# Value sums of a stick-breaking attention packed into column halves and quarters of the TensorE array

## The chip, the cores and the metric

The kernel runs on one core of one Trainium2 chip. The metric is the device time of one execution in microseconds (us); less is better. Of the engines, TensorE (PE) multiplies matrices, with its weight loads shown apart (PEld); VectorE (DVE), ScalarE (ACT) and GpSimd (POOL) work elementwise, and SyncE (SP) issues the transfers.

## The reference

One inference step of a two-layer decoder trunk, in fp32, for a prompt of 1024 positions and for 8 sample sequences of 8 new positions each, which share one set of weights. The width is 1024. Each layer is a normed token mixer and a SwiGLU channel mixer of width 2816. The mixer of the first layer has a convolution part (width 31, 512 channels) and a stick-breaking attention with 8 heads of 64, whose outputs are concatenated into one output projection. The second layer's mixer (a short convolution and causal pooling) is not touched here.

The attention has no softmax. With `z = q k / 8 + bias` and the strictly causal mask, the weight of key j for a query is `sigmoid(z_j)` times the product of `1 - sigmoid(z_m)` over the later keys m that the query sees. In the reference:

```python
log_1m = jnp.where(mask, jax.nn.log_sigmoid(-z), 0.0)
after = lax.cumsum(log_1m, axis=3, reverse=True) - log_1m
wgt = jnp.exp(jnp.where(mask, jax.nn.log_sigmoid(z) + after, -jnp.inf))
return jnp.einsum('nhqk,nkhd->nqhd', wgt, v)
```

The prompt attends to itself. Each sample attends to 1024 past positions, whose keys and values lie in 8 pages of 128 positions of a paged cache, and to its own new positions. Besides the trunk's output, the keys, values and the last states are returned.

## The kernel before, in words

All 1088 positions (1024 of the prompt, 64 of the samples) lie channel-major: channels on the 128 partitions, positions along the free dimension. They go through the first layer in two groups: GA has positions 0 to 511, GB 512 to 1087, the samples' 64 among them. The large products are made with three matmuls on two-part operands (a rounded high part and the rest) of type float32r; `mm3` (L231) issues them, L235 is their line, and `block` (L311) makes one output tile of them.

**Background flows.** The attention and the convolution are Python generators that are advanced by one piece in each slot of the projections: `block` calls its slot after every two steps of its inner dimension, and `bg` (L341) takes the next piece. A `yield` therefore means: a stretch of projection matmuls goes here. All engines execute their instructions in the order in which they were issued. `flow_ab` runs the convolution and then the attention of GA while GB is projected; `flow_c` runs the attention of GB, and then the convolution of GB and the sample attention in turns, while the output projection and the channel mixer of GA go on.

**Prompt attention** (`attention`, L937). A unit is one head and one tile of 128 queries; there are 32 in each group, in the order of heads and, in a head, from the last query tile to the first. A tile i has i+1 key tiles: 4 to 1 in GA, 8 to 5 in GB. Four stages, each one unit behind the one before:
- `s1` makes the scores. The contraction holds both parts of an operand in 128 rows: a head's 64 rows with the high parts of keys, and the other 64 rows with the low parts; `qa` has the high part of the queries in both halves, and `qz` their low part in the head's 64 rows and zeros in the rest. Two matmuls (L982) for each block of up to 512 keys, then two sigmoids on ACT.
- `s2` multiplies the running products (DVE).
- `s3` transposes the weights in tiles of 128 x 128 (L1011) and copies them to `wt` (ACT).
- `s4` sums values: per key tile one fp32 matmul with the 64 value columns as weights, into `o2` of 64 partitions (L1020), then one ACT copy (L1021).

**Sample attention** (`sample`, L1051). Two samples with 8 heads and 8 positions each fill 128 rows; there are four such pairs `bp`. Keys come in 24 units, in 48 steps of the loop at L1246. In a step, `trans` is called twice for the next step (transposes of three or two key pages, L1115, a copy on ACT and a subtraction on DVE into `kth`, L1119), `score` makes four matmuls (L1138), `score_b` adds the two parts and takes the sigmoids. When a pair is scored, its running products, and the transposes of its weights (L1187, into `wts`), follow in the next steps. They are put on the dictionary `chain`, and `turned` then puts four entries on `pvq`, each of which is two calls of `pv` (L1202).
- `pv(i)` sums the values of one page number of both samples of the pair: two fp32 matmuls (L1210), each of 64 rows of weights' columns (8 heads x 8 positions of one sample) and 512 moving columns (all heads' values of the page), into the two halves of `o`. The matmul computes every head's values for every head's rows; the wanted blocks are picked afterwards by `fin` with the selection matrix `sel` (L1224). After the eighth page come the new positions (`vnew`, L1217) and the copy out of PSUM (L1219).
- Pages come by `page_to` (L595) on SP's queue, which reads the page number there; two buffers of `vst` hold the values, six of `kst` the keys.

Every even step takes one entry from `pvq` at its end:

```python
if pvq and (s % 2 == 0 or s >= len(steps)):
    pvq.pop(0)()
s += 1
yield 2
```

Of the kernel before, what the change touches and what calls it, by code (L numbers as in the profile page):

```python
# [8 lines left out]
F = mybir.dt.float32  # L9
# [20 lines left out]
def f32(ap):  # L30
    return ap.bitcast(F)
# [13 lines left out]
HALF = 512  # L45
# [12 lines left out]
def trunk_kernel(ctx, tc, x_prompt, x_sample, cache_k, cache_v, state_conformer, state_shortconv, state_pool,  # L58
# [878 lines left out]
    def attention(g):  # L937
# [3 lines left out]
        with ExitStack() as es_:  # L941
# [4 lines left out]
            qz = [pa.tile([128, HALF], FR, name=f"qz{i}") for i in range(2)]  # L946
            for i in range(2):
                pool.memset(f32(qz[i][64 - 64 * i:128 - 64 * i]), 0.0)
# [4 lines left out]
            def operands(h):  # L953
                hp, hh = divmod(h, 2)
                r, o = slice(hh * 64, hh * 64 + 64), slice(64 - hh * 64, 128 - hh * 64)
                k = kt_[h] = pa.tile([128, NKEY], FR, name="kt", bufs=2)
                q = qa[h] = pa.tile([128, HALF], FR, name="qa", bufs=2)
                ks, qs = kall[r, hp, 0:NKEY], qall[r, hp, g.c0:g.c0 + HALF]
                small.append(lambda: act.activation(k[r], ks, AF.Copy))
                small.append(lambda: act.activation(q[r], qs, AF.Copy))  # L960
                for c in range(0, NKEY, 512):
                    small.append(lambda c=c: dve.tensor_tensor(k[o, c:c + 512], ks[:, c:c + 512],
                                                               f32(k[r, c:c + 512]), op=OP.subtract))
                small.append(lambda: act.activation(q[o], qs, AF.Copy))
                small.append(lambda: dve.tensor_tensor(qz[hh][r], qs, f32(q[r]), op=OP.subtract))
# [7 lines left out]
            def s1(u):  # L973
# [6 lines left out]
                for b in range(nb):  # L980
                    for s, q in enumerate((qa[h], qz[h % 2])):
                        pe.matmul(z[:, b, :nm], q[:, (i - i0) * 128:(i - i0) * 128 + 128], kt_[h][:, b * w:b * w + nm],  # L982
                                  start=s == 0, stop=s == 1)
# [19 lines left out]
            def s3(u):  # L1003
                i = units[u][1]
                be = bt.pop(u)
                w = wt[u] = pa.tile([128, i1, 128], F, name="wt")
# [7 lines left out]
            def s4(u):  # L1014
                h, i = units[u]
                hp, hh = divmod(h, 2)
                w = wt.pop(u)
                o = op_.tile([64, 128], F, name="o2")
                for j in range(i + 1):
                    pe.matmul(o, vrow[h][:, j], w[:, j], start=j == 0, stop=j == i)  # L1020
                act.activation(qall[hh * 64:hh * 64 + 64, hp, i * 128:i * 128 + 128], o, AF.Copy)  # L1021
# [7 lines left out]
            for u in range(len(units) + 3):  # L1029
                if u >= 3:  # L1030
                    s4(u - 3)
# [19 lines left out]
    def sample():  # L1051
# [5 lines left out]
        with ExitStack() as es_:  # L1057
# [144 lines left out]
            def pv(i):  # L1202
                bp, k = divmod(i, 8)
                if k == 0:
                    osum[bp] = op_.tile([128, 512], F, name="o")
                o = osum[bp]
                load_v(i + 1)
                for b2 in range(2):
                    r = slice(64 * b2, 64 * b2 + 64)
                    pe.matmul(o[r], wts[bp][:, k, r], vst[i][:, b2], start=k == 0, stop=False)  # L1210
# [4 lines left out]
                for b2 in range(2):  # L1215
                    r = slice(64 * b2, 64 * b2 + 64)
                    pe.matmul(o[r], wts[bp][:, 8, r], vnew, start=False, stop=True)  # L1217
                ob = tmp()[:, 0:512]
                act.activation(ob, o, AF.Copy)  # L1219

                def fin():
                    m = ms()
                    for hp in range(4):
                        pe.matmul(m[:, hp * 32:hp * 32 + 32], ob[:, hp * 128:hp * 128 + 128],  # L1224
# [21 lines left out]
            while s < len(steps) or chain or pvq or fins:  # L1246
# [6 lines left out]
                if s < len(steps):  # L1253
                    yield 1 if todo else 2
# [4 lines left out]
                if s < len(steps):  # L1259
                    yield 2  # L1260
# [15 lines left out]
                if pvq and (s % 2 == 0 or s >= len(steps)):  # L1276
                    pvq.pop(0)()
# [711 lines left out]
```

## Time and profile before

| | us |
|---|---|
| median of 3 runs | 2574.82 (2574.1 to 2576.08) |
| the profiled execution | 2575.97 |
| its span, first to last instruction | 2574.2 |
| PE busy | 2477.7 (96%) |
| DVE busy | 1693.0 (66%) |
| POOL busy | 1564.2 (61%) |
| ACT busy | 1105.3 (43%) |
| value sums of the prompt (L1020), first to last start | 238.2 to 563.7, 576 instructions |
| value sums of the samples (L1210), first to last start | 679.4 to 923.5, 128 instructions |

How to read it: in the profile's groups a line gives the source line, the engine, the operation, what is written and read, its shape, a count, and behind the bar the busy time, the mean duration in ns, the idle time ahead of it and who ended that. `128*64` of a matmul is rows times columns of its weights, and `128x512` what streams. In the timeline a row has the start, the time from the first start to the last end of the merged instructions, and their count. Matmuls overlap, so the duration of one is longer than its turn; turns are read as differences of starts. In the list of waits a row has who waited for whom, the total, the number and the longest.

### The profile page before, as it was taken

The numbers are of one execution on the slowest core, as the hardware profiler recorded it, in microseconds if no ns is written. First come the engines' busy times: TensorE is split into PE (matmuls) and PEld (weight loads), VectorE is DVE, ScalarE is ACT, GpSimd is POOL, SyncE is SP. The second block draws the span as 40 slices with busy tenths as digits, with TensorE's granted clock in tenths as the row PEclk, the third lists the DMA queues.
The fourth block names the chain that finished last, engine by engine and source line by source line (L and its number), as shares of the span: only waits on it lengthen the run. The fifth ranks groups of instructions, "written<-read, shape, count | busy, mean of one in ns | idle before, by whom it ended". The sixth has DMA issues, their size and how long they took to land.

```text
span 2574.2 us, 41142 instructions
## 1 busy us (share of the span) xinstructions
PE 2477.7 (96%) x15727; PEld 2213.7 (86%) x15727; DVE 1693.0 (66%) x2359; ACT 1105.3 (43%) x1875; POOL 1564.2 (61%) x1205
## 2 busy tenths in 40 slices
PE   8999999999999999999999999999999998999998
PEld 6788877887777668989999889989888887999997
DVE  3696777968867734467666633348776778666655
ACT  5536766754444334334333522234434434443333
POOL 6754243544434346678777722266888885887775
PEclk9999999999999999999999999999999999999999
DMA  7342231224555434222323411152233332333322
GB/s 220 113 113 74 64 109 46 70 83 142 157 162 160 139 107 152 74 74 83 99 83 98 130 42 46 38 161 65 84 91 96 95 96 82 107 95 103 99 83 78
DMA packets 355484, 258.30 MB, mean 100 GB/s; under 512 B 22913, under 2 KB 303617, under 8 KB 355272
## 3 DMA queue, kind: packets, MB, share of 16 engines
q1 hardware_dynamic: 355256, 255.66, 33.8%
q8 instruction: 125, 2.05, 0.3%
q14 instruction: 71, 0.58, 0.1%
q10 hardware_dynamic: 32, 0.01, 0.0%
HBM read 237.41 MB, written 18.69 MB: 99 GB/s over the span
## 4 chain that ended last, share of the span: by engine, by line
PE 44%; DVE 8%; POOL 2%; issue 1%; ACT 1%; POOLq 0%; DVEq 0%; ACTq 0%
PE acc L235 23%; PE acc L521 20%; POOL hl L197 1%; DVE sum L200 1%; DVE hid L241 1%; DVE hb L295 1%; DVE sum L201 1%; DVE b L1669 0%; DVE tmp L525 0%; DVE sum L202 0%; DVE x L1669 0%; DVE sum_c L214 0%; DVE fb L1673 0%; DVE xs L1673 0%; POOL tmp L500 0%
## 5 line engine op out<-in xcount | busy, mean ns | idle before, releaser
L186 POOL TENSOR_TENSOR hl<-stage,hl 128x512 fp32r<-128x512 f32 x464 | 634.7, 1391 | 475.1 <-ACT hl L184 357.0
L235 PE MATMUL acc<-x,hl 128*128 128x512 f32 (+1 forms) x3648 | 780.6, 350 | 12.2 <-DVE hb L295 2.6
L235 PEld LDWEIGHTS acc<-x,hl 128*128 128x128 f32 x3648 | 581.4, 189 | 77.2 <-issue 10.9
L235 PE MATMUL acc<-hid,hl 128*128 128x288 f32 (+1 forms) x3096 | 552.3, 334 | 16.8 <-DVE hb L295 6.9
L235 PEld LDWEIGHTS acc<-hid,hl 128*128 128x128 f32 x3096 | 470.4, 190 | 69.9 <-DVE hb L295 11.0
L295 DVE TENSOR_TENSOR hb<-acc,hb 128x512 f32<-128x512 f32 (+1 forms) x360 | 256.4, 718 | 184.8 <-PE acc L235 183.4
L521 PE MATMUL acc<-x,hl 128*128 128x288 f32 (+1 forms) x2676 | 362.4, 290 | 6.0 <-ACT x L1792 2.0
L521 PEld LDWEIGHTS acc<-x,hl 128*128 128x128 f32 x2676 | 349.0, 188 | 8.4 <-POOL hl L197 2.7
L197 POOL TENSOR_TENSOR hl<-sum,hl 128x512 fp32r<-128x512 f32 x180 | 237.1, 1344 | 168.6 <-ACT hl L196 168.5
L184 ACT ACTIVATE hl<-stage 128x1024 fp32r<-128x1024 f32 x232 | 243.5, 1055 | 218.5 <-PE acc L235 129.6
L525 DVE TENSOR_TENSOR tmp<-acc,tmp 128x288 f32<-128x288 f32 (+1 forms) x420 | 173.5, 441 | 228.0 <-ACT tmp L537 135.3
L197 POOL TENSOR_TENSOR hl<-stage,hl 128x512 fp32r<-128x512 f32 x180 | 267.0, 1505 | 13.3 <-ACT hl L196 13.3
L521 PE MATMUL acc<-b,hl 128*128 128x256 f32 (+1 forms) x1548 | 216.6, 291 | 14.1 <-DVE tmp L525 11.2
L521 PEld LDWEIGHTS acc<-b,hl 128*128 128x128 f32 x1548 | 202.3, 189 | 19.6 <-ACT hl L196 12.7
L235 PE MATMUL acc<-x1t,hl 128*128 128x288 f32 x1152 | 216.4, 296 | 1.5 <-POOL hl L186 1.5
L235 PEld LDWEIGHTS acc<-x1t,hl 128*128 128x128 f32 x1152 | 196.0, 188 | 19.4 <-POOL hl L186 1.7
L196 ACT ACTIVATE hl<-sum 128x512 fp32r<-128x512 f32 x180 | 103.1, 623 | 237.9 <-DVE sum L202 217.6
L291 DVE TENSOR_TENSOR tmp<-acc,rr 128x512 f32<-128x512 f32 (+1 forms) x108 | 75.0, 709 | 113.2 <-PE acc L235 100.0
L500 POOL TENSOR_TENSOR tmp<-tmp 128x576 f32<-128x576 f32 (+1 forms) x85 | 127.8, 1504 | 11.7 <-ACT tmp L477 8.3
L196 ACT ACTIVATE hl<-stage 128x512 fp32r<-128x512 f32 x180 | 105.6, 618 | 67.5 <-PE acc L235 62.3
L241 DVE TENSOR_TENSOR hid<-tmp,hid 128x512 fp32r<-128x512 f32 (+1 forms) x88 | 99.1, 1127 | 44.0 <-ACT hid L240 41.2
L235 PE MATMUL acc<-x1a,hl 128*128 128x512 f32 x480 | 121.7, 407 | 2.5 <-POOL hl L186 1.3
(289 smaller groups left out, 3242.9 us busy)
## 6 DMA issues: line engine op xcount, KB each, us to landing
stage<-in_w_ffn_in_dram SPq DMA_DIRECT2D x176, 512.0 KB
stage<-in_w_ffn_out_dram SPq DMA_DIRECT2D x88, 512.0 KB
stage<-in_w_in_even_dram SPq DMA_DIRECT2D x40, 512.0 KB
kst<-in_cache_k_dram SPq DMA_DIRECT2D x64, 256.0 KB
vst<-in_cache_v_dram SPq DMA_DIRECT2D x64, 256.0 KB
stage<-in_w_out_even_dram SPq DMA_DIRECT2D x16, 512.0 KB
stage<-in_w_in_odd_dram SPq DMA_DIRECT2D x16, 512.0 KB
stage<-in_w_out_odd_dram SPq DMA_DIRECT2D x16, 512.0 KB
```

Source lines behind the costliest of these rows:

```text
L184: act.activation(hl[:, 0], st, AF.Copy)
L186: pool.tensor_tensor(hl[:, 1, c], st[:, c], f32(hl[:, 0, c]), op=OP.subtract)
L196: act.activation(hl[:, 0, c], x, AF.Copy)
L197: pool.tensor_tensor(hl[:, 1, c], x, f32(hl[:, 0, c]), op=OP.subtract)
L200: todo = [lambda: dve.tensor_tensor(sb, su[:, lo], su[:, hi], op=OP.add), lambda: dve.tensor_tensor(sa[:, hi], sg[:, lo], su[:, lo], op=OP ...
L235: pe.matmul(acc[:, b, :c1 - c0], w, xs[:, xi, c0 - o:c1 - o], start=first and s == 0, stop=last and s == 2)
L241: (on or dve).tensor_tensor(dst[:, 1], src, f32(dst[:, 0]), op=OP.subtract)
L291: dve.tensor_tensor(d, a, r, op=OP.mult)
L295: dve.tensor_tensor(d, a, d, op=OP.add)
L500: (dve if both and f == NF - 1 else pool).tensor_tensor(t[:, :n], t[:, :n], u[:, :n], op=OP.mult)
L521: pe.matmul(acc[:, :w2], h[:, wi, i, k], xk[:, xi], start=k == 0 and s == 0, stop=k == 3 and s == 2)
L525: dve.tensor_tensor(out, acc[:, :w2], x, op=OP.add)
```

## The change

Four edits. The second score matmul of the prompt takes only the head's 64 rows of `qz` and of the keys, so the zeros and one of the two `qz` tiles go. `s4` is called for every second unit and sums two query tiles of a head in turns, one into partitions 0 to 63 of `o2` and one into 64 to 127; the transposed weights have two buffers, `wt0` and `wt1`. `pv` cuts each sample's 64 columns in two of 32, each with the 256 value columns of its four heads, so that one page number is four matmuls into four groups of 32 partitions; `o`, its copy and the operand of the selection are half as wide. And in the loop of the sample steps an entry of `pvq` is taken at odd steps, between the two calls of `trans`, and with nothing due in the step the `yield` between them moves behind them.

```diff
--- before.py
+++ after.py
@@ -943,9 +943,7 @@
             zp = es_.enter_context(tc.tile_pool(name=f"zp{g.c0}", bufs=1, space=PSUM, side="right"))
             op_ = es_.enter_context(tc.tile_pool(name=f"op{g.c0}", bufs=1, space=PSUM, side="right"))
 
-            qz = [pa.tile([128, HALF], FR, name=f"qz{i}") for i in range(2)]
-            for i in range(2):
-                pool.memset(f32(qz[i][64 - 64 * i:128 - 64 * i]), 0.0)
+            qz = pa.tile([128, HALF], FR, name="qz")
             kt_, qa, vrow, small = {}, {}, {}, []
 
 
@@ -962,7 +960,7 @@
                     small.append(lambda c=c: dve.tensor_tensor(k[o, c:c + 512], ks[:, c:c + 512],
                                                                f32(k[r, c:c + 512]), op=OP.subtract))
                 small.append(lambda: act.activation(q[o], qs, AF.Copy))
-                small.append(lambda: dve.tensor_tensor(qz[hh][r], qs, f32(q[r]), op=OP.subtract))
+                small.append(lambda: dve.tensor_tensor(qz[r], qs, f32(q[r]), op=OP.subtract))
 
             def load_v(h):
                 vrow[h] = pa.tile([128, i1, 64], F, name="vrow", bufs=2)
@@ -978,8 +976,9 @@
                 nm = max(w, 256)
                 z = zp.tile([128, 1 if g is GA else 2, 512], F, name="z2")
                 for b in range(nb):
-                    for s, q in enumerate((qa[h], qz[h % 2])):
-                        pe.matmul(z[:, b, :nm], q[:, (i - i0) * 128:(i - i0) * 128 + 128], kt_[h][:, b * w:b * w + nm],
+                    r = slice(h % 2 * 64, h % 2 * 64 + 64)
+                    for s, (q, k) in enumerate(((qa[h], kt_[h]), (qz[r], kt_[h][r]))):
+                        pe.matmul(z[:, b, :nm], q[:, (i - i0) * 128:(i - i0) * 128 + 128], k[:, b * w:b * w + nm],
                                   start=s == 0, stop=s == 1)
                 q = qt[u] = pa.tile([128, NKEY], F, name="q2", bufs=2)
                 be = bt[u] = pa.tile([128, NKEY], F, name="be", bufs=2)
@@ -1003,7 +1002,7 @@
             def s3(u):
                 i = units[u][1]
                 be = bt.pop(u)
-                w = wt[u] = pa.tile([128, i1, 128], F, name="wt")
+                w = wt[u] = pa.tile([128, i1 - u % 2, 128], F, name=f"wt{u % 2}")
                 for j0 in range(0, i + 1, 4):
                     n = min(4, i + 1 - j0)
                     m = ms().rearrange("p (j n) -> p j n", j=4)
@@ -1014,11 +1013,14 @@
             def s4(u):
                 h, i = units[u]
                 hp, hh = divmod(h, 2)
-                w = wt.pop(u)
-                o = op_.tile([64, 128], F, name="o2")
-                for j in range(i + 1):
-                    pe.matmul(o, vrow[h][:, j], w[:, j], start=j == 0, stop=j == i)
-                act.activation(qall[hh * 64:hh * 64 + 64, hp, i * 128:i * 128 + 128], o, AF.Copy)
+                ws = wt.pop(u - 1), wt.pop(u)
+                o = op_.tile([128, 128], F, name="o2")
+                for j in range(i + 2):
+                    for b in range(2 if j <= i else 1):
+                        pe.matmul(o[64 * b:64 * b + 64], vrow[h][:, j], ws[b][:, j], start=j == 0, stop=j == i + 1 - b)
+                for b in range(2):
+                    c = (i + 1 - b) * 128
+                    act.activation(qall[hh * 64:hh * 64 + 64, hp, c:c + 128], o[64 * b:64 * b + 64], AF.Copy)
 
             load_v(0)
             operands(0)
@@ -1027,7 +1029,7 @@
             for _ in range(3):
                 yield 1
             for u in range(len(units) + 3):
-                if u >= 3:
+                if u >= 3 and u % 2 == 0:
                     s4(u - 3)
                 if 2 <= u < len(units) + 2:
                     s3(u - 2)
@@ -1202,26 +1204,26 @@
             def pv(i):
                 bp, k = divmod(i, 8)
                 if k == 0:
-                    osum[bp] = op_.tile([128, 512], F, name="o")
+                    osum[bp] = op_.tile([128, 256], F, name="o")
                 o = osum[bp]
                 load_v(i + 1)
-                for b2 in range(2):
-                    r = slice(64 * b2, 64 * b2 + 64)
-                    pe.matmul(o[r], wts[bp][:, k, r], vst[i][:, b2], start=k == 0, stop=False)
+                for t in range(4):
+                    r, c = slice(32 * t, 32 * t + 32), slice(256 * (t % 2), 256 * (t % 2) + 256)
+                    pe.matmul(o[r], wts[bp][:, k, r], vst[i][:, t // 2, c], start=k == 0, stop=False)
                 vst.pop(i)
                 load_v(i + 3)
                 if k < 7:
                     return
-                for b2 in range(2):
-                    r = slice(64 * b2, 64 * b2 + 64)
-                    pe.matmul(o[r], wts[bp][:, 8, r], vnew, start=False, stop=True)
-                ob = tmp()[:, 0:512]
+                for t in range(4):
+                    r, c = slice(32 * t, 32 * t + 32), slice(256 * (t % 2), 256 * (t % 2) + 256)
+                    pe.matmul(o[r], wts[bp][:, 8, r], vnew[:, c], start=False, stop=True)
+                ob = tmp()[:, 0:256]
                 act.activation(ob, o, AF.Copy)
 
                 def fin():
                     m = ms()
                     for hp in range(4):
-                        pe.matmul(m[:, hp * 32:hp * 32 + 32], ob[:, hp * 128:hp * 128 + 128],
+                        pe.matmul(m[:, hp * 32:hp * 32 + 32], ob[:, hp % 2 * 128:hp % 2 * 128 + 128],
                                   sel[:, hp].rearrange("p b x -> p (b x)"), start=True, stop=True)
                     mv = m[:, 0:128].rearrange("p (h b y q) -> p h b y q", h=4, b=2, y=2)
                     c0 = SEQ + 16 * bp
@@ -1250,13 +1252,17 @@
                     f()
                 if s + 1 < len(steps):
                     trans(*steps[s + 1], 0)
-                if s < len(steps):
-                    yield 1 if todo else 2
+                if pvq and not soon and (s % 2 or s >= len(steps)):
+                    pvq.pop(0)()
+                if todo and s < len(steps):
+                    yield 1
                 if s + 1 < len(steps):
                     trans(*steps[s + 1], 1)
                 while soon:
                     soon.pop(0)()
                 if s < len(steps):
+                    if not todo:
+                        yield 2
                     yield 2
                 if s < len(steps):
                     u, pr = steps[s]
@@ -1273,8 +1279,6 @@
                             chain.setdefault(s + d, []).append(f)
                         chain.setdefault(s + (4 if bp < 3 else 5), []).append(
                             lambda bp=bp: turned(bp))
-                if pvq and (s % 2 == 0 or s >= len(steps)):
-                    pvq.pop(0)()
                 s += 1
                 yield 2
 
```

## The prediction

> **What bounds the kernel now.** I read the page first: its busy shares, then the granted clock in its slices.
>
> ```profile
> span 2574.2 us, 41142 instructions
> PE 2477.7 (96%) x15727; PEld 2213.7 (86%) x15727; DVE 1693.0 (66%) x2359; ACT 1105.3 (43%) x1875; POOL 1564.2 (61%) x1205
> PEclk9999999999999999999999999999999999999999
> ```
>
> TensorE has work almost all the time, and its granted clock does not move. The change touches three stretches, found from the first and last starts of its lines: the prompt attention of the first half (226 to 367 us), of the second half (380 to 567), and the sample attention (567 to 935). The same count by stretch:
>
> ```profile
> 226.00:367.00 141.00, 132.86 (x881) 114.83 (x880) 103.59 (x141) 101.85 (x212) 42.08 (x65) 0.99 0.32 88
> 380.00:567.00 187.00, 183.27 (x1058) 149.10 (x1058) 147.73 (x137) 121.98 (x196) 80.92 (x74) 1.00 0.20 55
> 567.00:935.00 368.00, 348.69 (x1661) 259.26 (x1660) 268.89 (x440) 144.13 (x295) 147.86 (x113) 0.99 0.52 152
> ```
>
> The columns after the length are PE, weight loads, DVE, ACT and POOL. PE is 94, 98 and 95% busy, DVE 73, 79 and 73%. So here a microsecond of TensorE is a microsecond of the kernel, as long as DVE keeps up. The list of waits of TensorE from 560 to 930 says how near DVE is:
>
> ```profile
> PE m L1115 <- DVE kth L1119: 4.8, 4, 2.4
> PE z L1138 <- DVE zs L1149: 3.5, 3, 2.1
> ```
>
> Four and three waits, and no engine's work that holds the whole stretch. Because a busy matmul is shown longer than its turn (matmuls overlap), I price everything below from start to start.
>
> **Part 1: prompt value sums in two column halves.** How many there are, from the groups by form, and the one-line view of the scores:
>
> ```profile
> L1020 PE MATMUL o<-wt,vrow 128*64 128x128 f32 x576 | 76.6, 278 | 0.0
> L1210 PE MATMUL o<-vst,wts 128*64 128x512 f32 x128 | 39.3, 657 | 3.0 <-DMA vst<-in_cache_v_dram 1.6 <-ACT wts L1188 1.3
> L1217 PE MATMUL o<-vnew,wts 128*64 128x512 f32 x16 | 5.0, 596 | 0.0
> L982 PE MATMUL z<-kt,qz x96: 278/339/766, 230.6 to 550.8; 128*128 128x512 f32 x24, 128*128 128x384 f32 x24, 128*128 128x256 f32 x16, 128*128 128x448 f32 x16
> ```
>
> A head has 1+2+...+8 = 36 value matmuls, eight heads 288; the trace has 576, so an fp32 matmul is two instructions. One clump, with a short and a long one in the timeline of PE:
>
> ```profile
> 301.97 0.30 PE L235 MATMUL acc<-x,hl 128*128 128x288 f32 x1
> 302.19 1.09 PE L1020 MATMUL o<-wt,vrow 128*64 128x128 f32 x8
> 303.21 0.55 PE L1011 MATMUL m<-ident,be 128*128 128x128 f32 x3
> 303.52 0.36 PE L982 MATMUL z<-kt,qa 128*128 128x256 f32 x1
> ...
> 546.19 1.96 PE L1020 MATMUL o<-wt,vrow 128*64 128x128 f32 x16
> 548.08 0.98 PE L1011 MATMUL m<-ident,be 128*128 128x128 f32 x7
> ```
>
> Eight take 1.02 us (302.19 to 303.21), sixteen 1.89: 0.109 each, one after the other, plus 0.15 for the clump. Ahead of it the last projection matmul holds 0.22 where its neighbours hold 0.13 (below, 181.99 to 182.25 for two): +0.09. Behind it three transposes take 0.31 where three elsewhere take 0.25 (below, 584.22 to 584.47): +0.06. A clump therefore costs 0.30 beside its matmuls, and there are 64, one for each unit of head and query tile.
>
> After the change two units share a clump and alternate between the column halves. That two halves really run at once is seen in the sample value sums, which already alternate between two halves:
>
> ```profile
> 773.67 0.51 PE L1138 MATMUL z<-kth,qb 128*128 128x384 f32 x2
> 774.12 1.94 PE L1210 MATMUL o<-vst,wts 128*64 128x512 f32 x8
> 775.99 1.67 PE L235 MATMUL acc<-x,hl 128*128 128x512 f32 x6
> 777.49 0.38 PE L1115 MATMUL m<-ident,kst 128*128 128x128 f32 x2
> ...
> 582.13 0.86 PE L1138 MATMUL z<-kth,qb 128*128 128x384 f32 x4
> 582.83 1.56 PE L235 MATMUL acc<-hid,hl 128*128 128x512 f32 x6
> 584.22 0.49 PE L1115 MATMUL m<-ident,kst 128*128 128x128 f32 x3
> 584.47 0.71 PE L235 MATMUL acc<-hid,hl 128*128 128x512 f32 x2
> ```
>
> At 0.109 per 128 columns, eight of 512 columns would take 8 × 0.436 = 3.5 us; they take 1.87, which is 4 × 0.436 plus a clump's 0.13. So pairs overlap fully. Per head the pairs of tiles then need 4+2 turns in the first half and 8+6 in the second, twice for the two instructions: 40 × 8 = 320 turns in place of 576. Saved: 256 × 0.109 = 27.9 us, and 32 clumps × 0.30 = 9.6. **Minus 37.5 us.** If the halves overlapped not at all, 9.6 alone is left. The two ACT copies out of PSUM stay 64 in number; the second tile's weights wait one unit longer in their own buffer, which nobody else writes.
>
> **Part 2: the second score matmul over 64 rows.** It streams the same columns as before, so nothing is gained on TensorE; two POOL memsets for each half are saved, off the path. But 96 matmuls that were 128 rows deep become 64 deep, each between full ones: with two PSUM blocks (second half) the order is full, half, full, half. The trace has 64-row matmuls in the transposes at the start, the last of a group of five, and a group of five without one:
>
> ```profile
> 59.82 0.47 PE L695 MATMUL m<-ident,xt 128*128 128x128 f32 x2
> 60.03 0.27 PE L695 MATMUL m<-ident,xt 64*128 64x64 f32 x1
> 60.23 3.07 PE L235 MATMUL acc<-x1a,hl 128*128 128x512 f32 x12
> 63.14 0.38 PE L695 MATMUL m<-ident,xt 128*128 128x128 f32 x2
> ...
> 181.99 0.42 PE L235 MATMUL acc<-x,hl 128*128 128x288 f32 x2
> 182.25 0.60 PE L773 MATMUL m<-ident,kall 128*128 128x128 f32 x4
> 182.68 0.27 PE L777 MATMUL m<-ident,kall 128*64 128x128 f32 x1
> ```
>
> A full transpose holds 0.11 (182.25 to 182.68 for four); the one ahead of the 64-row one holds 0.20 or 0.21: +0.10. The 64-row one of 64 columns, worth 0.05, holds 0.20: +0.15. The twelve matmuls behind it take 2.91, where six take 1.39 at 582.83, so twelve 2.78: +0.10, the little more being the spread of these rows. An excursion to 64 rows thus costs 0.35 us as it stands. It reads as two pauses of 0.10 to empty the array and two weight loads that nothing hides. The first load is a transpose's (0.05, as behind the value sums); a score's will be like the one that a projection matmul pays behind a clump: 775.99 to 777.49 is 1.50 for six against 1.39, so 0.10. I take 0.39: 96 × 0.39 = **plus 37.4 us**. Bounds: nothing, since the narrow transpose at 182.68 (64 columns, all rows) follows at the even pace; 0.45 at the upper end, 43 us. I take a value near the upper end because that row is 64 columns wide and not 64 rows deep. A gain is excluded: the same columns stream.
>
> **Part 3: sample value sums in four column quarters.** A clump now: entry 0.10 (773.67 to 774.12 is 0.45 for two scores, four at 582.13 take 0.70, so two 0.35), 1.87, exit 0.11: 2.08, of which four turns of 0.436 are 1.74 and 0.34 is the clump's own. After: 16 instructions of 256 columns, in four groups of four that run at once: 4 × 0.218 = 0.87, with the clump 1.21. Twelve clumps stand in the steady part: 12 × 0.87 = 10.4. The value rows of the new tokens (16 instructions in all, two turns a batch pair) go from 0.87 to 0.44: 1.3 for the three steady pairs of samples. The last four clumps, which follow each other with no transposes between them, wait for their pages:
>
> ```profile
> 914.04 1.43 PE L1210 MATMUL o<-vst,wts 128*64 128x512 f32 x4
> 915.68 2.21 PE L1210 MATMUL o<-vst,wts 128*64 128x512 f32 x4 [0.21 <-DMA vst<-in_cache_v_dram]
> 917.82 1.67 PE L235 MATMUL acc<-x,hl 128*128 128x512 f32 x6
> ```
>
> This one takes 3.78 us in place of 1.87. There a faster sum only frees its two page buffers sooner, by 0.44 a page; I count 0.5 for a clump, 2 in all (between 0 and 4). **Minus 13.7 us.** Bounds: nothing, if only two instructions ever run at once as the rows show (16 turns of 0.218 by two are the old 1.74); 17.
>
> A page bears on this size. The Trainium skill, "TensorE: Matmul & The Clock Gate", Part 3, gives three column tiles a measured speedup of 2.38, that is 0.79 of the ideal. No run here shows three or four; the two here reach all of two. By that efficiency, as an estimate, this part would be near minus 9 and the whole near minus 8 in place of minus 12.
>
> **Part 4: the sample step's new order.** In steps with nothing due, both groups of transposes and the value sums stand in one slot. Merging gains nothing by itself: three transposes at 584.22 take 0.25, and the matmul behind them only 0.09 more. The number of slots stays. The two transposes' PSUM buffers come round at the same distance of a step, and the score gets two slots behind the second transpose in place of one. The four page loads of each double value sum move on SP's queue ahead of the step's key loads, and a load that waits for its buffer holds key pages and weights behind it; both wait for the same stretch of TensorE as now, and TensorE shows no wait for weights there. Costed at nothing. The last value sums start one step later, which covers the 1.3 us wait for ACT (wts, in the row of L1210 above) and adds a slot: nothing.
>
> **The sum.** −37.5 + 37.4 − 13.7 = −13.8. DVE is at 73% where TensorE gets 4% faster, and its waits above (8 us) should grow by some of it: +1.5. In all −12.3. The profiled execution took 2575.97 us, 1.15 above the median of the runs, so 2563.7 there and 2562.5 beside the median.
>
> **The rivals.**
> - *The row change is cheap.* If what costs at 60.03 belongs to transposes, or scores pause less (0.29 and below), part 2 is 0 to 28 us: 2525 to 2553. For it: a single shape as witness. Against: the same pauses of 0.09 to 0.10 stand at every clump of another shape.
> - *Quarters go two by two.* Each value matmul is two instructions on the same quarter, in sequence; overlap beyond two needs more of them waiting at once than any row shows. Then part 3 is nothing: 2574 to 2577.
> - *Slower: the prompt halves do not overlap.* Their turns are 0.109 and each needs its own weights; the seen overlap had 0.436 to hide them. If a pair takes two turns, 9.6 is left of part 1: 2575 − 9.6 + 37.4 − 12.2 = 2590. It decides from the point where part 1 gives less than 25 of its 37.5 us.
> - *DVE takes it.* The conv taps and key splits share DVE with TensorE's next score; if its waits grow by 8 or more, 2570 to 2573. Against: the new order gives the key split a slot more.
>
> **How the numbers follow.** A step of 0.2% (5 us) is about what a measurement of this kernel can tell from no change. Forecast: 0.45, its own range 2555 to 2569. Row change cheap: 0.15. Two by two: 0.2. Slower: 0.12, with 0.03 more for an excursion above 0.53 us ((37.5 + 13.7) / 96). DVE: 0.05. Faster is the first two, 0.60; same is two by two and DVE, 0.25; slower 0.15. The range runs from 2546 (an excursion of 0.25 and part 3 at its upper bound) to 2579 (two by two, an excursion of 0.42); it leaves out the slower case and the row change at next to no price.
>
> **What would show it.** In the changed kernel's trace: 32 prompt value clumps, the longest with 30 instructions in about 1.9 us; scores of 64 rows with a start 0.20 or more after their neighbour's turn and the same behind them; sample clumps of 1.0 us from first start to the next line's, with four starts together; and no new long wait of TensorE on DVE from 560 to 930. The prediction is wrong if the 64-row scores follow without pause, or if 16 quarter instructions take 1.87 us as the 8 halves do.

## The result and the profile after

| | before | after |
|---|---|---|
| median, us | 2575.38 (2574.1 to 2578.63, 6 runs) | 2567.05 (2563.55 to 2570.58, 6 runs) |
| ratio of the times, with its 95% interval | | 0.9967 (0.9957 to 0.9977) |
| span of the profiled execution, us | 2574.2 | 2566.7 |
| its mean granted clock | 0.994 | 0.991 |

The change makes the kernel 8.3 us faster. The forecast was 12.3, with 2546 to 2579 as its range. The page of the changed kernel, its first lines and the granted clock:

```profile
span 2566.7 us, 41423 instructions
PE 2467.6 (96%) x15871; PEld 2196.0 (86%) x15871; DVE 1695.6 (66%) x2359; ACT 1106.1 (43%) x1875; POOL 1562.3 (61%) x1201
PEclk9999999999999999999999999999999999999999
```

The page looks like that of before: PE at 96%, DVE at 66%, the clock all nines. What changed is seen in the groups by form:

```profile
L1020 PE MATMUL o<-wt,vrow 128*64 128x128 f32 x576 | 41.8, 278 | 0.0
L1212 PE MATMUL o<-vst,wts 128*32 128x256 f32 x256 | 21.4, 394 | 5.7 <-DMA vst<-in_cache_v_dram 4.7 <-ACT wts L1190 0.7
```

The same 576 prompt matmuls hold 41.8 us of the array in place of 76.6, with the same 278 ns for one: two run at once. The sample matmuls are twice as many, and hold 21.4 in place of 39.3. The timeline of PE shows a prompt clump, and behind it a pair of scores with their 64-row halves (line numbers have moved by one or two):

```profile
370.76 1.96 PE L1020 MATMUL o<-wt,vrow 128*64 128x128 f32 x30
372.65 0.88 PE L1010 MATMUL m<-ident,be 128*128 128x128 f32 x6
...
374.77 0.39 PE L981 MATMUL z<-kt,qa 128*128 128x512 f32 x1
375.09 0.50 PE L981 MATMUL z<-kt,qz 64*128 64x512 f32 x1
375.52 0.49 PE L981 MATMUL z<-kt,qa 128*128 128x512 f32 x1
375.94 0.49 PE L981 MATMUL z<-kt,qz 64*128 64x512 f32 x1
376.36 1.67 PE L235 MATMUL acc<-x,hl 128*128 128x512 f32 x6
377.87 0.71 PE L1010 MATMUL m<-ident,be 128*128 128x128 f32 x5
```

Thirty instructions in 1.89 us, the time that sixteen took. The four scores hold 1.59 us (374.77 to 376.36). At the pace of a projection matmul of 512 columns, 0.232 to 0.235, they would hold 0.94: 0.65 too much. The six projection matmuls behind them hold 1.51 in place of 1.39: 0.12 more. So two excursions to 64 rows cost 0.77, one 0.39. The same view at a sample clump:

```profile
777.79 1.07 PE L1212 MATMUL o<-vst,wts 128*32 128x256 f32 x16
778.79 0.44 PE L1117 MATMUL m<-ident,kst 128*128 128x128 f32 x2
```

Sixteen quarter instructions in 1.00 us, which is four turns of 0.217 and a clump's 0.13. The starts come in fours, 7 ns apart (777.786, 777.793, 777.799, 777.806, and the next at 778.026). Four really run at once.

The windows cut at the same pieces of work in both kernels, before first, then after (the clock is the third column from the end):

```profile
224.00:388.00 164.00, 155.86 (x1024) 134.29 (x1024) 125.49 (x159) 118.33 (x239) 55.37 (x77) 0.99 0.30 84
388.00:564.00 176.00, 172.27 (x996) 139.81 (x995) 139.87 (x133) 115.29 (x185) 73.09 (x68) 1.00 0.19 53
564.00:934.00 370.00, 350.69 (x1669) 260.88 (x1670) 268.66 (x440) 145.45 (x297) 148.44 (x114) 0.99 0.52 151
934.00:2574.00 1640.00, 1587.44 (x10887) 1499.34 (x10885) 1018.40 (x1416) 624.04 (x1010) 1145.24 (x830) 0.99 0.30 90
```

```profile
224.00:391.00 167.00, 160.32 (x1011) 128.83 (x1010) 124.82 (x158) 119.47 (x237) 54.71 (x73) 0.97 0.29 81
391.00:569.00 178.00, 173.19 (x1012) 124.99 (x1011) 136.98 (x134) 116.59 (x186) 71.47 (x68) 0.99 0.19 54
569.00:931.00 362.00, 335.43 (x1814) 263.14 (x1814) 272.86 (x440) 144.32 (x298) 147.79 (x114) 0.98 0.53 155
931.00:2567.00 1636.00, 1587.04 (x10885) 1499.74 (x10884) 1018.95 (x1416) 624.04 (x1010) 1146.93 (x830) 0.99 0.30 90
```

The prompt attention is 5 us longer than before, the sample attention 8 us shorter. The last stage, in which no code changed, differs by 4 between these two executions, with the same clock; TensorE's waits there sum to 43.9 and 39.8. A single profile says nothing about so little, and the medians carry the total. The prompt's first window has 0.97 for the clock where it had 0.99. The slices of the page, 64 us each and in tenths, hide what that is. A window on it, and the timeline around it:

```profile
364.10:367.50 3.40, 3.33 (x12) 2.97 (x13) 3.33 (x3) 1.09 (x2) 2.78 (x3) 0.50 0.44 108
```

```profile
364.17 1.73 PE L1010 MATMUL m<-ident,be 128*128 128x128 f32 x7 [2.67 <-DVE be L1000]
365.55 2.52 PE L235 MATMUL acc<-x,hl 128*128 128x512 f32 x6
367.91 0.31 PE L981 MATMUL z<-kt,qa 128*128 128x320 f32 x1
```

TensorE waits 2.67 us for DVE. Then it gets half its clock for 3.40 us, and the six projection matmuls take 2.36 us in place of 1.39. From 224 to 930 such windows add up to 13.6 us before and 27.3 after, each behind a wait.

### The profile page after: what moved, and what is told of

Its sections match the earlier page's. It is cut to its first block, busy times and chain, and to the rows that moved or that the text cites. A ratio compares the mean times of both kernels' runs of the same rounds, so it can differ in the third digit from the quotient of the medians.

```text
span 2566.7 us, 41423 instructions
## 1 busy us (share of the span) xinstructions
PE 2467.6 (96%) x15871; PEld 2196.0 (86%) x15871; DVE 1695.6 (66%) x2359; ACT 1106.1 (43%) x1875; POOL 1562.3 (61%) x1201
## 4 chain that ended last, share of the span: by engine, by line
PE 45%; DVE 8%; POOL 2%; issue 1%; ACT 1%; POOLq 0%; DVEq 0%; ACTq 0%
PE acc L235 24%; PE acc L521 20%; POOL hl L197 1%; DVE hid L241 1%; DVE sum L200 1%; DVE sum L201 1%; DVE hb L295 1%; DVE b L1673 0%; DVE tmp L525 0%; DVE sum_c L214 0%; DVE sum L202 0%; DVE fb L1677 0%; PE blk L1896 0%; DVE x L1673 0%; POOL tmp L500 0%
## 5 line engine op out<-in xcount | busy, mean ns | idle before, releaser
L186 POOL TENSOR_TENSOR hl<-stage,hl 128x512 fp32r<-128x512 f32 x464 | 638.1, 1399 | 461.1 <-ACT hl L184 336.4
L197 POOL TENSOR_TENSOR hl<-stage,hl 128x512 fp32r<-128x512 f32 x180 | 267.1, 1505 | 13.3 <-ACT hl L196 13.3
L500 POOL TENSOR_TENSOR tmp<-tmp 128x576 f32<-128x576 f32 (+1 forms) x85 | 127.6, 1501 | 16.3 <-ACT tmp L477 8.3
```

The costliest lines, as they stand in the source:

```text
L186: pool.tensor_tensor(hl[:, 1, c], st[:, c], f32(hl[:, 0, c]), op=OP.subtract)
L197: pool.tensor_tensor(hl[:, 1, c], x, f32(hl[:, 0, c]), op=OP.subtract)
L500: (dve if both and f == NF - 1 else pool).tensor_tensor(t[:, :n], t[:, :n], u[:, :n], op=OP.mult)
```

## The experiments

The time of the unchanged kernel is the median of the runs beside each experiment. Ratios are to it, with 95% intervals.

**The rows alone.** The kernel before, with only the second score matmul over 64 rows:

```diff
-for s, q in enumerate((qa[h], qz[h % 2])):
-    pe.matmul(z[...], q[...], kt_[h][...], ...)
+for s, (q, k) in enumerate(((qa[h], kt_[h]), (qz[r], kt_[h][r]))):
+    pe.matmul(z[...], q[...], k[...], ...)
```

> The kernel before with the 64-row second score matmul alone. Theory (every change between 128 and 64 rows empties the array and bares a weight load, 0.39 us for each of the 96 matmuls, as the trace of the changed kernel shows between starts): 37 us slower than before, 2612 to 2614, ratio 1.0145. Rival (the pauses stand in slack that DVE or a buffer gives anyway): the trace shows the pauses, but the time grows by less than 20 us. Rival (the row change is nearly free and what is seen in the changed kernel comes from its neighbours): within 5 us of before.

2608.09 beside 2576.07, ratio 1.0120 (1.0105 to 1.0134): plus 32 us. The timeline of PE at two of its excursions:

```profile
500.81 0.31 PE L981 MATMUL z<-kt,qa 128*128 128x320 f32 x1
501.04 0.41 PE L981 MATMUL z<-kt,qz 64*128 64x320 f32 x1
...
502.06 1.67 PE L235 MATMUL acc<-x,hl 128*128 128x512 f32 x6
```

Four scores hold 1.25, where 320 columns each are worth 0.15, 0.59 in all. Over all 64 units the scores hold 68.9 us where they held 38.8; with the 0.11 to 0.12 behind each unit's last one, the pauses add up to the forecast 37 us. TensorE's waits in the prompt stretches fell from 11.5 to 7.2 us meanwhile: the pauses give DVE time, and that is most of the 5 us between 37 and 32.

**The excursions grouped.** The changed kernel, with all full-row scores of a unit ahead of all its 64-row ones. That takes away 32 of 96 excursions and no work:

```diff
-for b in range(nb):
-    for s, (q, k) in enumerate(...):
+for s, (q, k) in enumerate(...):
+    for b in range(nb):
```

> The changed kernel with the scores of a unit reordered: all full-row matmuls of the unit first, then all 64-row ones, so that the 32 units of two blocks change mode once instead of twice. Theory (the price is for the change of mode, 0.39 us for one excursion): 32 excursions fewer, 12.5 us faster than the changed kernel, about 2554.5, ratio to before 0.992. Rival (the price is for each 64-row matmul): the same as the changed kernel, 2567.

2558.03 beside 2576.07, 0.9930 (0.9917 to 0.9942): 9 us less than the changed kernel. Its timeline of PE, in a unit of the same size as the one above:

```profile
502.75 0.46 PE L981 MATMUL z<-kt,qa 128*128 128x320 f32 x2
503.14 0.56 PE L981 MATMUL z<-kt,qz 64*128 64x320 f32 x2
503.62 1.67 PE L235 MATMUL acc<-x,hl 128*128 128x512 f32 x6
```

The scores hold 0.87 where they held 1.25. Over all units the scores hold 56.2 us in place of 68.2 in the changed kernel, 12.0 less, as expected (32 × 0.39 = 12.5), but TensorE's waits in the prompt grow from 11.4 to 14.8. The price hangs on the number of switches and not on the number of 64-row matmuls.

**The quarters alone.** The kernel before, with `pv` of the changed one (and what `fin` picks, to fit), and the slots in the old order:

> The kernel before with the value sums of the samples in quarters alone, in the old order of the step. In the changed kernel the value sums lost 18 us on TensorE and the sample stretch only 8. Theory A (the new order gives it back: the transposes of the new weights' column and of the convolution's state wait for the two PSUM buffers): without the new order the stretch keeps 13 us or more, 2560 to 2563, ratio 0.995. Theory B (DVE gives it back whatever the order): 8 us, 2567, ratio 0.997.

2566.11 (2561.19 to 2572.04) beside 2576.07, 0.9962 (0.9947 to 0.9977): minus 10 us. In its profile the sample stretch is 357.5 us long in place of 370. That is nearer to theory B: most of the loss is there without the new order too, as the next run confirms.

**The order alone.** The kernel before, with only the new place of `pvq` and of the `yield`:

> The kernel before with the new order of the sample step alone (value sums in halves). Theory (two PSUM buffers serve three transposes in one slot, so the transposes of the new weights' column and of the convolution's state wait, some 0.6 us three times and 1 to 2 us once or twice): 2 to 5 us slower than before, 2578 to 2581, with these waits in the trace. Rival (the order costs nothing, as predicted): within 1.5 us.

2574.22 beside 2575.40 (12 and 20 runs), 0.9998 (0.9989 to 1.0008): nothing. The theory of a loss fell. Its waits from 564 to 940:

```profile
PE m L888 <- DVE kth L1119: 2.7, 2, 1.9
...
PE m L1187 <- DVE bet L1173: 1.2, 1, 1.2
PE z L1138 <- DVE zs L1149: 1.0, 1, 1.0
```

A new wait of 2.7 us (L888, transposes of the background convolution) is real, but that for `bet` falls from 2.7 to 1.2, and that for `zs` from 3.5 to 1.0.

**Full rows back.** The changed kernel, with the second score over 128 rows as before. The two whole tiles of `qz` have no room beside `wt0` and `wt1`, so four tiles of 128 columns hold the low parts, each made by a small DVE subtraction one unit ahead:

```diff
-dve.tensor_tensor(qz[r], qs, f32(q[r]), op=OP.subtract)          # 16 in all
+dve.tensor_tensor(qz[hh][u % 2][r], qall[...128 columns], f32(qa[h][r, c:c + 128]), op=OP.subtract)   # 64 in all
```

> The changed kernel with full-row second score matmuls again. The two tiles with zeros of before do not fit beside the second buffer of weights (43.5 KB of 42.2 for a partition), so the low part is made for one query tile at a time, in four tiles of 128 columns, by 64 small subtractions on DVE in place of 16 large ones. Theory: all 96 excursions go, 96 x 0.396 = 38 us faster than the changed kernel, less some us for the small subtractions: 2527 to 2534, ratio 0.983. Rival (the pauses hide waits for DVE that come back): under 25 us faster, 2542 or more, with new waits of TensorE on DVE in the two attention stretches.

2549.83 beside 2576.07, 0.9895 (0.9880 to 0.9909): minus 17 us against the changed kernel, where the pauses alone would give 37. The waits of PE from 220 to 575, and the group of subtractions on DVE:

```profile
PE m L1021 <- DVE be L1011: 15.9, 12, 3.5
```

```profile
L972 DVE TENSOR_TENSOR qz<-hb,qa 64x128 fp32r<-64x128 f32 x64 | 37.4, 585 | 1.0
```

The wait for the running products was 3.2 us in the changed kernel and is 15.9 here. Its 12.7 us are more than half of the 20 that are missing. DVE has 37.4 us of these subtractions where the changed kernel has 16.5, which could be the cause by itself; the next two look at that.

**Half as many subtractions, and the key splits on POOL.** First two tiles of 256 columns, 32 subtractions, and the old order of the sample step. Then the same with the 24 key splits moved. And the kernel before, with only the key splits moved:

```diff
-small.append(lambda c=c: dve.tensor_tensor(k[o, c:c + 512], ks[:, c:c + 512],
+small.append(lambda c=c: pool.tensor_tensor(k[o, c:c + 512], ks[:, c:c + 512],
```

> Halves for the prompt, quarters for the samples, full-row scores, the old order of the step. The low part of the queries is made for two query tiles at a time in two tiles of 256 columns (32 subtractions on DVE). Theory (without the 64-row scores the attention's units are shorter than DVE's chain of scans and products, so TensorE waits for it, and each wait of some us halves its clock for 3.4 us more; the first full-row kernel had small subtractions that made this worse): 2540 to 2547, that is 3 to 10 us faster than the first one, with waits of L1011's kind on DVE still there. Rival (only the small subtractions were to blame): 2533 or less.

> The same with the splitting of the keys on POOL, which takes some 17 us from DVE in the two attention stretches. Theory (DVE is what the prompt's gain was lost to): 5 us or more faster than with the keys on DVE, 2532 to 2540, with fewer waits on DVE and a higher granted clock. Rival (POOL's own lateness, or DVE slowed by POOL beside it, takes it back): no faster than with the keys on DVE.

> The kernel before with the splitting of the prompt's keys on POOL in place of DVE (24 subtractions of 64x512, some 17 us of DVE). A control: theory (before the change DVE keeps up, so relief of DVE alone gains little): within 4 us of before. Rival (DVE is a bound of the attention already): 8 us faster or more.

2550.25, 0.9903 (0.9889 to 0.9918), for the first. 2553.05, 0.9915 (0.9902 to 0.9928), for the second. 2581.28, 1.0026 (1.0014 to 1.0037), for the third; all beside 2575.40. All three came out slower than their theories. Fewer subtractions do not shorten the waits (first kernel, then the second, PE from 223 to 550):

```profile
PE m L1020 <- DVE be L1010: 16.3, 12, 3.5
```

```profile
PE m L1020 <- DVE be L1010: 17.0, 14, 3.4
PE acc L235 <- POOL hl L186: 4.3, 1, 4.3
PE z L990 <- POOL kt L962: 2.4, 2, 2.0
```

So the number of subtractions is not the cause: halving them took 10 us of busy time from DVE in the prompt (279 to 269) and changed nothing. POOL takes 1562 to 1582 ns for a key split that takes DVE 801 to 807 in the mean, and behind it stand the projections' operands (`hl`, L186): the move brings waits of its own, and 6 us of loss in the kernel before. Nor does it relieve DVE. The windows of the prompt (first kernel, then the second; DVE is the third busy time):

```profile
223.00:550.00 327.00, 300.59 (x2025) 253.49 (x2025) 268.68 (x307) 234.49 (x424) 130.29 (x145) 0.97 0.25 71
223.00:554.00 331.00, 302.98 (x2031) 255.66 (x2029) 267.76 (x285) 234.96 (x423) 166.53 (x169) 0.96 0.25 70
```

DVE has 24 subtractions (18.6 us) fewer and is busy for only 0.9 us less: its other instructions take longer, the scan of 128 x 128 for example 0.76 us in the mean in place of 0.65. That DVE's instructions are longer beside POOL's is seen in the kernel before: of its 40 subtractions of 64 x 512 on DVE, 30 take 0.68 to 0.69 us, one 1.04 and nine 1.56 to 1.77; these ten overlap with POOL's operations for 1.1 us or more, 28 of the 30 for at most 0.1. So the rival holds (DVE slowed by POOL beside it), and moving the splits cannot tell whether DVE is short of time.

**The weights one slot later.** The first of the three, with `s3` of the second half issued behind the slot's projection matmuls, which gives DVE that much longer. The same edit on the changed kernel is the control:

```diff
-if 2 <= u < len(units) + 2:
+if g is GA and 2 <= u < len(units) + 2:
     s3(u - 2)
 ...
     yield 1
+    if 2 <= u < len(units) + 2:     # GB only
+        s3(u - 2)
```

> Halves, quarters, full-row scores, old order of the sample step, low part for two query tiles at a time, and in the second half of the prompt the transposes of a unit one slot later (behind the yield). Theory (with two units in one value clump every second unit has no clump, so its transposes come up to 2 us earlier than DVE's scans and product can follow; the 64-row pauses had filled that): most of the 11 waits of 14 us in the second half go, and the half-speed clock behind them; 8 to 13 us faster than the kernel without the shift, 2537 to 2542, ratio 0.986. Rival (DVE is short of time, not late): the waits move to another instruction and nothing is gained, 2550.

> The changed kernel with the same shift of the transposes. A control: there the 64-row scores lengthen each unit by 0.8 us and the second half has 3 waits of 4.5 us, so at most 3 to 5 us are to be had: 2562 to 2567. Rival (the shift is good by itself, for another reason): 2558 or less.

2544.25 beside 2576.46, 0.9877 (0.9862 to 0.9893): 6 us less than without the edit, where 8 to 13 were expected. The control has 2565.50, 0.9963 (0.9949 to 0.9976), as the changed kernel has. The wait that the edit aims at, from 220 to 550:

```profile
PE m L1020 <- DVE be L1010: 10.0, 9, 2.4
```

16.3 became 10.0, and 6 us of time went. All of it lies behind 337 us, in the second half, where the edit is: there 13.9 became 7.6, and ahead of it 2.4 stayed 2.4. The time at half clock did not fall with it (17.1 us in the prompt in both profiles). This is the best kernel here that computes everything: 32 us faster than before, 23 faster than the change.

**Less work on DVE.** The first of the three again, with the 24 key splits left out: the low parts of the keys are zeros from POOL, so this computes with the keys' high parts alone.

```diff
-small.append(lambda c=c: dve.tensor_tensor(k[o, c:c + 512], ..., op=OP.subtract))
+small.append(lambda c=c: pool.memset(f32(k[o, c:c + 512]), 0.0))
```

> The kernel with full-row scores, halves, quarters and the old order, without the splitting of the prompt's keys: the low parts of the keys are left out (set to zero by POOL), which takes 24 subtractions, some 20 us, from DVE and leaves TensorE's work as it is. Theory (DVE's time in the attention is what TensorE waits for once the 64-row pauses are gone): 8 us or more faster than the 2550 of that kernel, with the waits for DVE in the attention at half or less. Rival (the order of a unit's steps is late, not DVE short): under 4 us, waits as before.

2535.31 (2532.89 to 2541.35) beside 2575.12, 0.9845 (0.9826 to 0.9864): 15 us less than the first of the three, for 24 subtractions that held DVE for 18.6. The wait and the window of the prompt (from 223 to 540):

```profile
PE m L1019 <- DVE be L1009: 9.6, 11, 2.1
```

```profile
223.00:540.00 317.00, 300.47 (x2053) 254.59 (x2052) 253.21 (x285) 235.75 (x426) 143.50 (x172) 0.99 0.27 75
```

The prompt takes 317 us in place of 327, and DVE is busy for 253 in place of 269. The wait falls from 16.3 to 9.6, not quite to the half that was expected. Time at half clock in the prompt stretches falls from 17.1 to 6.8 us, and the mean clock of the profile rises from 0.990 to 0.994. So the splits on DVE are part of what TensorE waits for once the pauses are gone. That DVE's load as a whole sets the wait is not shown: the 10 us that went with half of the small subtractions brought nothing, so it matters which work goes, and when it was due.

**Waits put in.** Does a wait bring the half clock, or does something else bring both? In the kernel before, far from the attention (the channel mixer of GB), twelve made-up waits of TensorE on DVE: six short, six long. They add work whose result nobody reads.

```diff
+if 130 <= j < 202 and (j - 130) % 6 == 0:
+    pe.transpose(m[:, 0:128], ident, ident)
+    ...                                  # 1 or 4 DVE operations on m, a copy to d
+    pe.transpose(m[:120, 0:128], d, ident)
```

> The kernel before with twelve added waits of TensorE in the channel mixer of the second group, 6 tiles of weights apart: six times it waits for about one short DVE chain (1.3 us), then six times for four times as long a one (3 us or more). Theory (a wait of some 2 us and more is followed by 3.4 us at half the clock, a short one is not): six or more new half-clock stretches in the second part and none or one in the first; a long wait costs its length and some 1.7 us. Rival (the half-clock stretches stand beside waits by chance): no more of them than before (none between 1150 and 1750 us), and the added time is the sum of the waits.

2616.75 beside 2576.46, 1.0168 (1.0147 to 1.0188). Five of the short waits came out at 1.1 to 1.7 us, and none of them is followed by a half clock; the first one fell into a stretch where this kernel waits anyway, and is 8.3 us there. Of the six long ones, 3.3 to 3.9 us, three are followed by it and three are not, where the theory had all six. A long one with it and one without, in the timeline:

```profile
1301.09 0.32 PE L232 MATMUL m<-ident,halo 128*120 128x128 f32 x1 [3.29 <-DVE halo L231]
...
1273.43 0.33 PE L232 MATMUL m<-ident,halo 128*120 128x128 f32 x1 [3.29 <-DVE halo L231]
```

Both waits are 3.29 us. What decides is where they lie. In each of the 14 profiles here the stretches at half clock begin at whole multiples of 3.413 us from each other, so the clock is set on a fixed row of windows, whatever the kernel does. Cut at these borders (PE's busy time is the first number behind the length, the clock the third from the end):

```profile
1299.06:1302.47 3.41, 1.38 (x11) 1.39 (x12) 3.31 (x7) 0.00 (x0) 0.00 (x0) 1.00 0.09 36
1302.47:1305.89 3.42, 3.42 (x17) 3.42 (x16) 2.02 (x5) 1.15 (x2) 2.25 (x2) 0.50 0.00 0
1268.34:1271.75 3.41, 1.79 (x14) 1.53 (x12) 1.51 (x3) 1.35 (x2) 2.92 (x4) 1.00 0.92 267
1271.75:1275.17 3.42, 1.74 (x13) 1.74 (x14) 3.20 (x7) 0.00 (x0) 2.24 (x2) 1.00 0.15 40
1275.17:1278.58 3.41, 3.41 (x28) 3.41 (x27) 0.82 (x2) 1.06 (x1) 0.41 (x1) 1.00 0.55 155
```

The first wait takes 2.0 us out of one window, which keeps 1.38 of work, and the next window has half the clock. The second wait lies across a border, each of the two windows keeps a little over half its work, and nothing follows. All profiles agree, counted from 100 us behind the start to 20 ahead of the end: behind a window at full clock in which TensorE was busy for less than 0.44 of the time, the next had half the clock in 90 of 90 cases; behind one with 0.56 or more, in none of 9637; in between it went both ways. So a wait brings the half clock, where nothing else of the kernel differs, if it leaves one of these windows less than about half busy.

## Why the prediction was right, and where its sizes were off

**Part 1, prompt halves** (forecast −37.5). From a clump's first start to the next line's, the 64 clumps held 78.0 us and the 32 clumps hold 41.8. TensorE was idle for 5.2 and 1.8 of these; without that it is 72.8 to 40.0, and with the 0.15 that a clump costs the lines beside it, −37.6. The halves overlap at turns of 0.109, so the slower rival (no overlap) fell. No run has this part alone.

**Part 2, 64 rows** (forecast +37.4, at 0.39 an excursion). The rows show 0.39, and the turns sum to about 37. The rival of a cheap row change fell. The Trainium skill, "TensorEngine Tiling (Array Packing)", section Key Properties, says that a change of the tiling mode drains the TensorE, and gives no price; the trace agrees in that a pause stands at each change, and has 0.39 us for there and back. How much of it is emptying and how much weight loads that nothing hides, the rows do not separate. The kernel with this edit alone bears the sign out, at 32 of the 37 us.

**Part 3, quarters** (forecast −13.7). From 43.6 to 25.6 us by the same measure, waits included: −18.0, and −10 by the medians where it was made alone. The twelve steady clumps went from 26.6 to 13.3, where 11.7 were counted off; one of them had stood at half clock before (3.19 us in place of 1.87). The last four, whose pages the forecast had at −2, gave −4.7, and one of these had stood at half clock too (3.42). So up to 3 of the 18.0 belong to the clock of that one execution. The rival "two by two" fell: four run at once. The estimate by the three column tiles of the Trainium skill, "TensorE: Matmul & The Clock Gate", Part 3, minus 8 for the whole, came near the measured −8.3, but not for its reason: four quarters lose nothing here.

**Part 4, the order** (forecast nothing): nothing, by the kernel that has it alone. One of its sentences was too simple: the two buffers also serve other transposes, hence the 2.7 us at L888, which other waits paid back.

**The last term, DVE** (+1.5), was mis-sized, and with it the statement that the granted clock does not move. The three large terms came to −18.6 (−37.6 + 37 − 18.0) in place of −13.8, the time to −8.3. So waits and clock took about 10 us by the medians. By the windows it is 5 + 37.6 − 37 = 6 in the prompt and 18.0 − 8 = 10 in the samples, 16 in all; the last stage, 4 shorter in this one execution, is not part of that. In the samples it is mostly waits, which went from 19.1 to 26.1 us:

```profile
PE m L1117 <- DVE kth L1121: 5.3, 3, 2.6
PE acc L235 <- DVE hb L295: 5.3, 5, 2.1
PE o L1212 <- DMA vst<-in_cache_v_dram: 4.7, 5, 1.3
```

(That is the list of PE from 226 to 940 in the changed kernel; for `hb` it was 3.2, for the pages 1.6.) In the prompt the sum of waits stayed at about 11 us (11.5 and 11.4), and the half-clock time grew from 3.4 to 13.6, worth up to half of the 10.2 more; about 1 us there, and 1 to 3 in the samples, have no owner. That waits on DVE bring such windows is shown by the waits put in; that the windows there cost exactly this is worked out, not measured. The clock moved in the kernel before too: the windows of 3.4 us at half clock add up to 13.6 us there, which the page's slices hid from the prediction. Its two prompt stretches were also cut late: the second half's first score starts at 347.1, not at 380. Nothing in the sum hangs on that.

The direction and the main steps held, and that the total came so near is in part luck, for two misses met: part 3 gave 4.3 more than forecast, and waits and clock took 9 to 14 more. The rival "DVE takes it" was thus half true, and it was given 0.05. It is larger without the 64-row scores: then DVE is late where the pauses had covered it, and of 37 us of pauses taken away only 17 arrive.

## What to carry to other kernels

Packing narrow matmuls into column halves and quarters gave its full factor here, even for turns of 0.11 us; a matmul over half the rows between full ones gave nothing and cost 0.39 us for each way there and back, so put such matmuls together, or pad them with zeros. Before counting a saved microsecond of a busy TensorE as one of the kernel, look at what its partner engine does in that stretch: beside a DVE that is 73 to 79% busy, half of a large saving did not arrive, most of it because of waits for DVE, and the next gain had to come from DVE's own work or from a later due time. Moving DVE's work to POOL was no relief here, as DVE's other instructions grew longer beside POOL's. Read the granted clock in windows of a few us around waits, not in the page's slices: a wait of 2 us can bring 3.4 us at half the clock.

## What the runs showed of the hardware that was not expected

- The granted clock falls to 0.50 for one window of 3.41 us, on a fixed row of such windows, behind one in which TensorE was busy for less than about half of the time (90 of 90 below 0.44, none of 9637 from 0.56 on). So of two waits of 3.29 us one brought it and one did not.

  The Trainium skill, "TensorE: Matmul & The Clock Gate", Part 1, section What's actually happening, has a free-running window of 3413 ns and half the clock after an idle one. The profiles agree with the length and with free-running; that a window which is only half idle is enough is not what the page says.
- Run to run, a kernel's time roughly follows its mean granted clock: the quarters alone took 2561 to 2564 us at 0.992 and 0.993, and 2572 at 0.989.
- Four fp32 matmuls on four column quarters start 7 ns apart and take one turn, 0.217 us for 256 columns.
- A DVE subtraction takes 0.68 us for 64 x 512 and 0.27 to 0.29 for 64 x 128 where POOL hardly works beside it, and mostly 1.6 to 1.8 and 1.2 to 1.4 beside a POOL operation. In the one-line views (shortest, median and longest in ns; the kernel before, then full rows):

```profile
L965 DVE TENSOR_TENSOR qz<-hb,qa x16: 677/689/1769, 229.8 to 523.8; 64x512 fp32r<-64x512 f32 x16
L972 DVE TENSOR_TENSOR qz<-hb,qa x64: 273/289/1382, 229.4 to 534.8; 64x128 fp32r<-64x128 f32 x64
```
